# A decoder step on one core: the sample's attention in even steps, with four 32-column tiles in place of two of 64

## The chip, the cores and the metric

The kernel runs on one core of a Trainium2 chip. The metric is the device time of one execution in microseconds (us), lower is better; the time of a kernel is the median of its runs. The engines of the core that appear below are TensorE (PE; its weight loads are listed apart as PEld), VectorE (DVE), ScalarE (ACT), GpSimd (POOL) and SyncE (SP, which here issues every DMA).

## The reference

One layer of a decoder for a prompt of 512 tokens and for a sample group of 8 sequences with 8 new tokens each, after 2048 past tokens. Both share the weights. All is float32.

```python
z = rms(x) @ w_in                               # 9776 columns: q, k/v, gates, RNN inputs
# A) sparse attention, 16 heads of 64, 4 key/value heads
k_c, v_c = compress(past, 32 -> 1)              # 64 compressed blocks of the past
o_cmp, imp = softmax(q @ k_c) @ v_c             # imp: which blocks matter
idx = top_k(imp, 15)                            # of 32 blocks of 64 keys
o_sel = softmax(q @ [k[idx], k_new]) @ [v[idx], v_new]
o_win = softmax(q @ [last 512 keys, k_new]) @ ...
o_att = g0 * o_cmp + g1 * o_sel + g2 * o_win    # gates per head
# B) RG-LRU recurrence; then both are projected, gated, merged, projected again
y = x + (sig(gm_att) * ((o_att * silu(g_att)) @ w_att_out) + sig(gm_rnn) * u_rnn) @ w_out
```

For the sample group, per sequence ("batch" below): 16 heads x 8 tokens = 128 query rows; 2048 past keys in pages of 128, of which the selected blocks count, 512 window keys and 8 new ones.

## The kernel before

**The main stream.** TensorE works through the weights in column tiles of 128. A slot is half the rows of such a tile for half of the 576 tokens: 8 steps of three matmuls, 24 in all (L1609 to L1611: each weight and each input is split into two parts, high and low, of the faster float32r type). ACT makes the high part of a weight (L225, `whi`), DVE the low one (L231, `wlo`), and SP loads the weight after the next (L218, `raw`) as soon as the low part is done. The remaining work of the kernel is inserted between slots, and, for the sample's attention, also in the middle of a slot.

**The order.** The program sets the order itself (`manual_schedule`): on each engine instructions stand as the code states them. The sample's attention is a list of events with a time each (`sample_events`, by the numbers of `SCH`); `sample_steps` executes those of one time and tells by a cost estimate how far it has come. `sample_work` calls it until that share catches up with the share of the slots that lie between the end of the prompt's attention and the RNN. It is called at the beginning and in the middle of each slot.

**One batch.** All 128 query rows share the partitions. Keys lie as [64 dims of two key heads, keys], so that a pair `c` of key heads is one matmul: its weights are 64 query columns (2 heads x 32 rows, zero where the head does not match), its moving side 256 keys (`s_scores`, L904). The pair c=0 writes partitions 0 to 63, c=1 64 to 127; these are the 64-column tiles. The operands are true float32, and such a matmul shows in the trace as two instructions, two passes.

- `c_square` to `x_select`: norm of the compressed keys, their scores (`m<-skvx,qb`), softmax, sum over heads (L930), choice of blocks as a bias per block.
- `k_load`, `v_load`: keys and values by pages, on SP's queue, in pieces of 256 keys.
- `k_scores`, `k_max`: scores of 512 keys (a "part", n2 = 0 to 3 past, 4 window) into a bank `s`; DVE adds the bias, copies to SBUF and takes the maximum.
- `s_softmax`, `s_exp`, `s_scale`, `p_scale`: when all five parts have their maxima, one maximum for each of the two softmaxes; ACT exponentiates; sums, reciprocal and gate make one factor per row, with which POOL scales the probabilities.
- `s_turn`, `s_turned`: four 128 x 128 transposes on TensorE (`t`, L1023), copied out by ACT (`spt`).
- `s_out`: probabilities (64 columns of a pair) times values (128 columns: both heads of the pair, of which each row needs one), L1052, all added up in one bank `o`, the new and compressed keys' first (`vx`).
- `s_sum`, `s_fin`, `s_put`: copy, transpose, and the wanted halves into `osm`.

A batch's scores begin 38 event times after its own beginning, its values 66, and batches follow every 22, so that values of one batch and scores of a later one alternate.

Of the kernel before, what the change touches and what calls it, by code (L numbers as in the profile page):

```python
# [10 lines left out]
F = mybir.dt.float32  # L11
# [5 lines left out]
VLAG = 2  # L17
KEPT = 3
NORM = 15
BASE = 2.0  # L20
# [5 lines left out]
CF, PG = 18, 25  # L26
YSTD = 4
SCH = 22, 38, 66, 5
# [13 lines left out]
TINY = 1e-30  # L42
# [5 lines left out]
def _constants():  # L48
# [26 lines left out]
    add("zero", np.zeros((128, 1)))  # L75
    return np.concatenate(cols, 1)
# [37 lines left out]
def nsa_rglru_step(ctx, tc, a, o):  # L114
# [714 lines left out]
    def q_batch(x):  # L829

        x.q = pp["s"].tile([128, 2, 64], F, tag="qb", name="qb", bufs=2)
        G.memset(x.q, 0.0)
        for c in range(2):
            for gl in range(2):
                me = slice(gl * 64, gl * 64 + 64)
                V.tensor_copy(x.q[me, c, gl * 32:gl * 32 + 32].rearrange("p (r t) -> p r t", t=8), zs[me, c, :, x.b:64:8])
# [29 lines left out]
    def c_reduce(x, n):  # L866
        if n == 0:
            x.kvx = pp["a"].tile([128, 4, 80], F, tag="skvx", name="skvx", bufs=3)
# [5 lines left out]
    def c_fetch(x):  # L874
        if x.b >= KEPT:
            x.kvx = pp["a"].tile([128, 4, 80], F, tag="skvx", name="skvx", bufs=3)
            S.dma_start(x.kvx[:, :, 8:72], kc_d[x.b])
# [23 lines left out]
    def s_scores(dst, x, k):  # L901

        for c in range(2):
            T.matmul(dst[c * 64:c * 64 + 64], x.q[:, c], k(c), start=True, stop=True)  # L904

    def x_scores(x):

        m = bank("m")
        s_scores(m[:, :80], x, lambda c: x.kvx[:, c, :])
        x.m = m  # L910

    def x_exp(x):
        m = held_bank("m", x.m)
        x.e = pp["s"].tile([128, 80], F, tag="se", name="se", bufs=3)
        x.sm = pp["s"].tile([128, 24], F, tag="ssm", name="ssm", bufs=3)
        sm = x.sm
        V.tensor_add(x.e[:, 0:8], m[:, 0:8], C("snew"))
        V.tensor_add(x.e[:, 72:80], m[:, 72:80], C("snew"))
        V.tensor_reduce(sm[:, 0:1], m[:, 8:72], axis=AX.X, op=OP.max, negate=True)
        A.activation(x.e[:, 8:72], m[:, 8:72], AF.Exp, bias=sm[:, 0:1], accum_out=sm[:, 1:2])  # L920

    def x_prob(x):
        sm = x.sm
        V.tensor_scalar_max(sm[:, 1:2], sm[:, 1:2], TINY)
        V.reciprocal(sm[:, 1:2], sm[:, 1:2])
        V.tensor_scalar_mul(x.e[:, 8:72], x.e[:, 8:72], sm[:, 1:2])

    def x_sum(x):
        m = bank("m")
        T.matmul(m[:, :64], C("rsum"), x.e[:, 8:72], start=True, stop=True)  # L930
        x.m = m

    def x_select(x):
# [12 lines left out]
        V.tensor_scalar_mul(x.e[:, 8:72], x.e[:, 8:72], gR[:, 0, x.b:x.b + 1])  # L946

    kraw, vraw = {}, {}

    def k_load(x, n):  # L950
        t = pp["s"].tile([128, 2, 256], F, tag="kr", name="kr", bufs=6)
        if n < 8:
            for k in range(2):
                S.dma_start(t[:, :, k * 128:k * 128 + 128],
                            a["selk"][ds(page(x.b, 2 * n + k, "k"), 1)].rearrange("o p c f -> p (o c) f"))
        else:
            S.dma_start(t, a["wink"][x.b, :, :, (n - 8) * 256:(n - 8) * 256 + 256])
        kraw[x.b, n] = t

    def v_load(x, n):  # L960
        t = ap.tile([128, 2, 256], F, tag="q", name="vr", bufs=8)
        if n < 8:
            for k in range(2):
                S.dma_start(t[:, k], a["selv"][ds(page(x.b, 2 * n + k, "v"), 1)].rearrange("o p f -> p (o f)"))
        else:
            S.dma_start(t, a["winv"][x.b, :, (n - 8) * 2:(n - 8) * 2 + 2])
        vraw[x.b, n] = t

    def k_scores(x, n2):

        x.s = bank("s")
        for n in (2 * n2, 2 * n2 + 1):
            t = kraw.pop((x.b, n))
            s_scores(x.s[:, n % 2 * 256:n % 2 * 256 + 256], x, lambda c: t[:, c])

    def k_max(x, n2):
        s, sm = held_bank("s", x.s), x.sm
        p = pp["s"].tile([128, 512], F, tag="p2", name="sp", bufs=2) if (x.b * 5 + n2) % 8 > 5 else \
            pp["a"].tile([128, 512], F, tag="p", name="sp", bufs=6)
        x.P[n2] = p  # L980
        if n2 < 4:
            V.tensor_tensor_reduce(p.rearrange("p (n k) -> p n k", k=64), s.rearrange("p (n k) -> p n k", k=64),
                                   x.bias[:, n2 * 8:n2 * 8 + 8, None].to_broadcast([128, 8, 64]), 1.0, -3.0e38,
                                   OP.add, OP.max, sm[:, 4 + n2:5 + n2])
        else:
            V.tensor_tensor_reduce(p[:, :8], s[:, :8], C("wm"), 1.0, -3.0e38, OP.add, OP.max, sm[:, 9:10])
            V.tensor_tensor_reduce(p[:, 8:], s[:, 8:], C("zero").to_broadcast([128, 504]), 1.0, -3.0e38, OP.add, OP.max, sm[:, 11:12])

    def s_softmax(x):

        sm, e = x.sm, x.e
        V.tensor_reduce(sm[:, 8:9], e[:, 0:8], axis=AX.X, op=OP.max)
        V.tensor_reduce(sm[:, 10:11], e[:, 72:80], axis=AX.X, op=OP.max)
        V.tensor_reduce(sm[:, 2:3], sm[:, 4:9], axis=AX.X, op=OP.max, negate=True)
        V.tensor_reduce(sm[:, 3:4], sm[:, 9:12], axis=AX.X, op=OP.max, negate=True)

    def s_exp(x, n2):
        sm, e = x.sm, x.e
        if n2 < 5:
            p = x.P[n2]  # L1000
            A.activation(p, p, AF.Exp, bias=sm[:, 3:4] if n2 == 4 else sm[:, 2:3],
                         accum_out=sm[:, 12 + n2:13 + n2] if n2 < 4 else sm[:, 17:18])
        else:
# [708 lines left out]
```

## Time and profile before

| | |
|---|---|
| median of 3 runs | 1703.17 us (1701.27 to 1703.93) |
| profiled execution | 1700.71 us, span 1698.9 us |
| TensorE busy | 1673.2 us (98%), 12645 matmuls |
| DVE / ACT / POOL busy | 1027.0 / 747.8 / 348.6 us |
| TensorE clock granted | 0.997 of full |
| HBM | 155 GB/s over the span |

The span is the time from the first to the last instruction; the execution's own time is 1.8 us more. Busy time counts instructions that overlap only once. A matmul's recorded duration includes its way through the array, so matmuls that start every 0.13 us each last about 0.3; how fast they follow each other is read from their starts. In a row of the timeline come start, duration, engine, line, operation, output and inputs, shapes, and how many equal instructions were put together. "Idle before" and "<-" name what an engine waited for. The sample's attention runs from about 723 to 1056 us of the span.

### The profile page before, as it was taken

What the parts mean: (1) busy time and instruction counts of PE and PEld (TensorE: products, weight loads), DVE (VectorE), ACT (ScalarE), POOL (GpSimd) and SP (SyncE); (2) the same over time, 40 slices, a digit from 0 to 9 for tenths busy, and PEclk for the clock granted to TensorE, in tenths of its full rate; (3) what the DMA queues carried; (4) which work ended last, traced back from release to release, by engine and by line L of the source; (5) the groups of instructions that cost most, each with busy time, mean ns of one, the idle gap of its engine ahead of it and who ended that gap; (6) DMA issues with size and microseconds to landing.
All of it is one profiled execution on the core that took longest, in us unless ns stands there. A gap on an engine that the chain in (4) does not pass through costs nothing.

```text
span 1698.9 us, 32907 instructions
## 1 busy us (share of the span) xinstructions
PE 1673.2 (98%) x12645; PEld 1599.3 (94%) x12645; DVE 1027.0 (60%) x2117; ACT 747.8 (44%) x1361; POOL 348.6 (21%) x423
## 2 busy tenths in 40 slices
PE   9989999999999999999999999999999999999999
PEld 8989999998998999988888889999999999999999
DVE  6767768778776876443333422656655334448785
ACT  6354553554455454343444432566664122233332
POOL 0014443533543444310011020000003011110000
PEclk9999999999999999999999999999999999999999
DMA  6247534533543444366676654322227444556442
GB/s 223 76 169 243 182 112 134 164 103 116 165 135 104 149 149 136 120 191 212 209 216 196 206 177 133 100 79 83 79 89 242 138 153 142 166 183 227 154 136 81
DMA packets 147455, 257.93 MB, mean 152 GB/s; under 512 B 19937, under 2 KB 80482, under 8 KB 147042
## 3 DMA queue, kind: packets, MB, share of 16 engines
q1 hardware_dynamic: 147298, 255.82, 46.6%
q8 instruction: 100, 1.64, 0.4%
q14 instruction: 57, 0.47, 0.1%
HBM read 228.08 MB, written 36.07 MB: 155 GB/s over the span
## 4 chain that ended last, share of the span: by engine, by line
PE 81%; DVE 10%; ACT 6%; issue 2%; DMA 1%; SPq 0%; POOL 0%; ACTq 0%; POOLq 0%; DVEq 0%
PE g L1609 21%; PE g L1610 20%; PE g L1611 20%; PE o L1052 3%; PE s L904 2%; DVE wlo L231 2%; PE g L1386 1%; PE g L1384 1%; PE g L1385 1%; PE t L737 1%; DVE pt L741 1%; DVE p L718 1%; ACT p L722 1%; ACT whi L225 1%; PE t L1023 1%
## 5 line engine op out<-in xcount | busy, mean ns | idle before, releaser
L1609 PE MATMUL g<-xh,whi 128*128 128x288 f32 x2368 | 716.5, 303 | 0.1
L1611 PE MATMUL g<-xh,wlo 128*128 128x288 f32 x2368 | 698.9, 295 | 1.1 <-DVE wlo L231 1.1
L1610 PE MATMUL g<-xl,whi 128*128 128x288 f32 x2368 | 699.1, 295 | 0.0
L1609 PEld LDWEIGHTS g<-xh,whi 128*128 128x128 f32 x2368 | 446.1, 188 | 22.2 <-issue 19.6
L1610 PEld LDWEIGHTS g<-xl,whi 128*128 128x128 f32 x2368 | 446.1, 188 | 1.3
L1611 PEld LDWEIGHTS g<-xh,wlo 128*128 128x128 f32 x2368 | 445.7, 188 | 1.3 <-DVE wlo L231 1.3
L231 DVE TENSOR_TENSOR wlo<-raw,whi 128x1024 fp32r<-128x1024 f32 x192 | 257.2, 1340 | 98.6 <-ACT whi L225 98.1
L225 ACT ACTIVATE whi<-raw 128x1024 fp32r<-128x1024 f32 x192 | 202.2, 1053 | 116.8 <-PE g L1610 111.9
L864 POOL TENSOR_TENSOR cr<-cr,wcs 128x512 f32<-128x512 f32 x128 | 182.8, 1433 | 158.4 <-DMA cr<-in_cmp 133.2
L722 ACT ACTIVATE p<-p,sm,rq 128x128 f32<-128x128 f32 (+3 forms) x128 | 82.8, 648 | 150.2 <-DVE sm L719 150.0
L730 POOL TENSOR_SCALAR p<-p,sm 128x128 f32<-128x128 f32 (+3 forms) x128 | 68.7, 549 | 211.9 <-DVE sm L727 94.7
L741 DVE TENSOR_TENSOR pt<-t,pt 128x512 fp32r<-128x512 f32 x96 | 66.1, 689 | 65.0 <-ACT pt L740 63.7
L870 DVE TENSOR_REDUCE skvx<-cr 128x16 f32<-128x512 f32 x128 | 86.7, 677 | 0.4
L1017 POOL TENSOR_SCALAR sp<-sp,ssm 128x512 f32<-128x512 f32 x40 | 30.9, 789 | 262.0 <-DVE ssm L1012 224.0
L740 ACT ACTIVATE pt<-t 128x512 fp32r<-128x512 f32 x96 | 56.5, 592 | 57.4 <-PE t L737 56.6
L571 ACT ACTIVATE mh<-ur 128x288 fp32r<-128x288 f32 x32 | 14.2, 445 | 145.0 <-POOL ur L565 145.0
L1611 PE MATMUL g<-oah,wlo 128*128 128x288 f32 x256 | 75.5, 295 | 0.0
L1611 PE MATMUL g<-hrh,wlo 128*128 128x288 f32 x256 | 75.5, 295 | 0.0
L1610 PE MATMUL g<-oal,whi 128*128 128x288 f32 x256 | 75.4, 295 | 0.0
L1609 PE MATMUL g<-oah,whi 128*128 128x288 f32 x256 | 75.4, 294 | 0.0
L1610 PE MATMUL g<-hrl,whi 128*128 128x288 f32 x256 | 75.3, 294 | 0.0
L1609 PE MATMUL g<-hrh,whi 128*128 128x288 f32 x256 | 75.3, 294 | 0.0
(377 smaller groups left out, 2967.5 us busy)
## 6 DMA issues: line engine op xcount, KB each, us to landing
raw<-in_w_in SPq DMA_DIRECT2D x152, 512.0 KB, 3.4
cr<-in_cmp SPq DMA_DIRECT2D x128, 256.0 KB, 3.4
kr<-in_selk SPq DMA_DIRECT2D x128, 128.0 KB, 3.1
vr<-in_selv SPq DMA_DIRECT2D x128, 128.0 KB, 3.4
tg<-gm SPq DMA_DIRECT2D x32, 288.0 KB, 4.4
tgi<-tg SPq DMA_DIRECT2D x32, 288.0 KB, 4.2
yr<-in_w_out SPq DMA_DIRECT2D x18, 512.0 KB, 4.7
raw<-in_w_rnn SPq DMA_DIRECT2D x16, 512.0 KB, 4.2
```

The source lines that it names most:

```text
L225: A.activation(hi, raw[k], AF.Copy)
L231: V.tensor_sub(lo, raw.pop(k), hi.bitcast(F))
L722: A.activation(p[:, :n], p[:, :n], AF.Exp, bias=sm[:, 1, r - r0:r - r0 + 1], scale=rq[:, i, r:r + 1], accum_out=sm[:, 2, r - r0:r - r0 + 1])
L730: G.tensor_scalar(p[:, :n], p[:, :n], sm[:, 3, r - r0:r - r0 + 1], 1.0, op0=OP.mult, op1=OP.mult)
L740: A.activation(hi, t, AF.Copy)
L741: V.tensor_sub(lo, t, hi.bitcast(F))
L864: G.tensor_tensor(v, v, wcs[:, :, None, :].to_broadcast([128, 4, 4, 32]), op=OP.mult)
L870: V.tensor_reduce(x.kvx[:, :, 8 + n * 4:12 + n * 4], v, axis=AX.X, op=OP.add)
L1052: T.matmul(ob[c * 64:c * 64 + 64, :128], pt[rows, k, c], v[rows, u, c * 128:c * 128 + 128], start=n < 0, stop=n == 9 and u == 1, skip_grou ...
L1609: T.matmul(gb[:, :HF], wh[:, k, :], r_h[:, hs], start=kk == 0, stop=False)
L1610: T.matmul(gb[:, :HF], wh[:, k, :], r_l[:, hs], start=False, stop=False)
L1611: T.matmul(gb[:, :HF], wl[:, k, :], r_h[:, hs], start=False, stop=last and k == 7)
```

## The change

Four things change together.

1. **Tiles.** The query weights become [128, 4, 32]: one key head each, with 32 query columns. `s_scores` issues four matmuls of 512 keys, whose results lie on partitions 0, 32, 64 and 96. `s_out` issues, for 128 keys, four matmuls of 32 columns with only the 64 value columns of that head. The result of a part is [128, 64].
2. **Softmax by parts.** Each part of 512 keys takes its own maximum (the negative, as a minimum) and is exponentiated at once, without waiting for the others. The values of each part go into their own 64 columns of bank `o`, eight in all: four past parts, new keys, window, window's new keys, compressed keys. At the end factors exp(max of part - max of all), times the gate and over the sum, weigh the eight (`s_factors`, `s_total`, `s_sum`). The scaling of probabilities on POOL is gone. The new and compressed keys' probabilities are turned in one go and masked into three copies (`x_turned`, constant `xm`), with three times four matmuls (`x_out`).
3. **Order.** `sample_steps` states 52 even steps: batch b starts at step 6 + 5b; part n2 is loaded three steps ahead (values: at the step itself), scored at t, turned at t + 2, and used at t + 3. Within a step the transposes come first, then the values, then the scores. `sample_work` is called once a slot, and a step is never split.
4. **Memory.** Keys come in tiles of 512 (4 buffers); the pool of the prompt's attention is closed before the sample's opens.

```diff
@@ q_batch
-        x.q = pp["s"].tile([128, 2, 64], F, tag="qb", name="qb", bufs=2)
+        x.q = pp["s"].tile([128, 4, 32], F, tag="qb", name="qb", bufs=3)
...
@@ s_scores
-        for c in range(2):
-            T.matmul(dst[c * 64:c * 64 + 64], x.q[:, c], k(c), start=True, stop=True)
+        for h in range(4):
+            T.matmul(dst[h * 32:h * 32 + 32], x.q[:, h], k(h // 2), start=True, stop=True)
...
+    def x_out(x):
+        ob = held_bank("o", x.o)
+        for n, part in enumerate((4, 6, 7)):
+            for h in range(4):
+                T.matmul(ob[h * 32:h * 32 + 32, part * 64:part * 64 + 64], x.pt[:80, n * 128 + h * 32:n * 128 + h * 32 + 32],
+                         x.pt[:80, 384 + h * 64:448 + h * 64], start=True, stop=True)
...
@@ k_load
-        t = pp["s"].tile([128, 2, 256], F, tag="kr", name="kr", bufs=6)
+        t = x.K[n2] = pp["s"].tile([128, 2, 512], F, tag="kr", name="kr", bufs=4)
...
@@ s_exp
-            A.activation(p, p, AF.Exp, bias=sm[:, 3:4] if n2 == 4 else sm[:, 2:3],
-                         accum_out=sm[:, 12 + n2:13 + n2] if n2 < 4 else sm[:, 17:18])
+        p, n = x.P[n2], n2 + n2 // 4
+        A.activation(p, p, AF.Exp, bias=x.sm[:, NM + n:NM + n + 1], scale=-1.0, accum_out=x.sm[:, SUM + n:SUM + n + 1])
...
-    def p_scale(x, n2):
-        G.tensor_scalar(x.P[n2], x.P[n2], x.sm[:, 23:24] if n2 == 4 else x.sm[:, 22:23], 1.0, op0=OP.mult, op1=OP.mult)
...
@@ s_out
-            for c in range(2):
-                T.matmul(ob[c * 64:c * 64 + 64, :128], pt[rows, k, c], v[rows, u, c * 128:c * 128 + 128],
-                         start=n < 0, stop=n == 9 and u == 1, skip_group_check=True)
+        for k in range(4):
+            for h in range(4):
+                T.matmul(ob[h * 32:h * 32 + 32, at_:at_ + 64], pt[:, k, h * 32:h * 32 + 32], v[k // 2][:, k % 2, h * 64:h * 64 + 64],
+                         start=k == 0, stop=k == 3)
...
@@ s_sum
-        x.t2 = etile("t2")[:, :128]
-        A.activation(x.t2, held_bank("o", x.o)[:, :128], AF.Copy)
+        V.tensor_mul(t, ob, x.sm[:, FAC:FAC + 8, None].to_broadcast([128, 8, 64]))
+        V.tensor_reduce(x.t2, t.rearrange("p n d -> p d n"), axis=AX.X, op=OP.add)
...
@@ sample_steps
+            s = 6 + 5 * x.b
...
+            for n2 in range(5):
+                t = s + n2
+                put(t - 3, 0, k_load, x, n2)
+                put(t, 0, v_load, x, n2)
+                put(t, 4, k_scores, x, n2)
+                put(t, 8, k_max, x, n2)
+                put(t, 9, s_exp, x, n2)
+                put(t + 2, 1, s_turn, x, n2)
+                put(t + 2, 6, s_turned, x, n2)
+                put(t + 3, 2, s_out, x, n2)
+            put(s + 3, 3, x_out, x)
...
@@ main loop
-                sample_work(s + 0.5)
+                sample_work(s + 1)
...
-            if step == 4 and ssteps is not None and s < slot_of[first_r]:
-                sample_work(s + 1)
```

How this moves instructions on TensorE, in the middle of the sample's attention. Before, values of one batch and scores of a later one; the rows left out are 12 projection matmuls each time:

```order
L1052 MATMUL o<-vr,spt 64x128 x4
L1023 MATMUL t<-cst,sp 128x128 x4
...
L1052 MATMUL o<-vr,spt 64x128 x4
L904 MATMUL s<-kr,qb 64x256 x4
L904 MATMUL m<-skvx,qb 64x80 x2
```

Now, about the same place; the rows left out are 24 projection matmuls:

```order
L1021 MATMUL t<-cst,sp 128x128 x4
L957 MATMUL t<-cst,se 80x128
L959 MATMUL t<-cst,skvx 80x128 x2
L1035 MATMUL o<-vr,spt 32x64 x16
L902 MATMUL s<-kr,qb 32x512 x4
...
L1021 MATMUL t<-cst,sp 128x128 x4
L887 MATMUL m<-ssq,cst 128x128
L1035 MATMUL o<-vr,spt 32x64 x16
L902 MATMUL s<-kr,qb 32x512 x4
```

Full-width transposes come first, and then all tiled matmuls of the step in one run, a whole slot apart from the next. (`order` names are those of the profile: `o`, `s`, `t`, `m` are banks, `vr` and `kr` values and keys, `spt` turned probabilities, `qb` queries.)

The second place is SP's queue, where the keys and values of a step are issued. Before (a row without tile names is a register instruction):

```order
L964 DMA vr<-in_selv 128x256
L954 ISA
L954 DMA kr<-in_selk 128x2x128
L954 ISA
L954 DMA kr<-in_selk 128x2x128
L218 DMA raw<-in_w_in 128x1024
L964 ISA
L964 DMA vr<-in_selv 128x256
```

Now:

```order
L991 ISA
L991 DMA vr<-in_selv 128x256
L981 ISA
L981 DMA kr<-in_selk 128x2x128
L981 ISA
L981 DMA kr<-in_selk 128x2x128
L981 ISA
L981 DMA kr<-in_selk 128x2x128
L981 ISA
L981 DMA kr<-in_selk 128x2x128
L216 DMA raw<-in_w_in 128x1024
```

Four value loads and four key loads of a step follow each other; a weight load, which waits for DVE's `wlo`, stands behind them and ahead of the next step's loads.

More of the change, by code (lines that the diff above doesn't have):

```diff
@@ L75, in _constants @@
     add("zero", np.zeros((128, 1)))
+    add("xm", np.stack([p < 8, (p >= 72) & (p < 80), (p >= 8) & (p < 72)], 1))
     return np.concatenate(cols, 1)
@@ L867, in c_reduce @@
         if n == 0:
-            x.kvx = pp["a"].tile([128, 4, 80], F, tag="skvx", name="skvx", bufs=3)
+            x.kvx = pp["x"].tile([128, 4, 80], F, tag="skvx", name="skvx", bufs=3)
         v = x.cr.pop(n).rearrange("p c (n j) -> p c n j", j=32)
@@ L875, in c_fetch @@
         if x.b >= KEPT:
-            x.kvx = pp["a"].tile([128, 4, 80], F, tag="skvx", name="skvx", bufs=3)
+            x.kvx = pp["x"].tile([128, 4, 80], F, tag="skvx", name="skvx", bufs=3)
             S.dma_start(x.kvx[:, :, 8:72], kc_d[x.b])
@@ new lines, in x_turn_, with x_turned @@
+    def x_turn_(x):
+        t = x.tx = bank("t")
+        T.transpose(t[:80, 0:128], x.e, ident)
+        for c in range(2):
+            T.transpose(t[:80, 128 + c * 128:256 + c * 128], x.kvx[:, 2 + c, :], ident)
+    def x_turned(x):
+        t = held_bank("t", x.tx)
+        x.pt = pp["s"].tile([128, 640], F, tag="vx", name="vx", bufs=2)
+        for n in range(3):
+            A.activation(x.pt[:80, n * 128:n * 128 + 128], t[:80, :128], AF.Copy, scale=C("xm")[:80, n:n + 1])
+        A.activation(x.pt[:80, 384:], t[:80, 128:384], AF.Copy)
@@ L954, in k_load @@
                 S.dma_start(t[:, :, k * 128:k * 128 + 128],
-                            a["selk"][ds(page(x.b, 2 * n + k, "k"), 1)].rearrange("o p c f -> p (o c) f"))
+                            a["selk"][ds(page(x.b, 4 * n2 + k, "k"), 1)].rearrange("o p c f -> p (o c) f"))
         else:
[L957 to L967, printed above, removed]
+            S.dma_start(t, a["wink"][x.b])
@@ L969, in k_scores, with v_load @@
+    def v_load(x, n2):
+        t = x.V[n2] = [ap.tile([128, 2, 256], F, tag="q", name="vr", bufs=8) for _ in range(2)]
+        for k in range(2):
+            if n2 < 4:
+                for i in range(2):
+                    S.dma_start(t[k][:, i], a["selv"][ds(page(x.b, 4 * n2 + 2 * k + i, "v"), 1)].rearrange("o p f -> p (o f)"))
+            else:
+                S.dma_start(t[k], a["winv"][x.b, :, 2 * k:2 * k + 2])
     def k_scores(x, n2):
         x.s = bank("s")
-        for n in (2 * n2, 2 * n2 + 1):
-            t = kraw.pop((x.b, n))
-            s_scores(x.s[:, n % 2 * 256:n % 2 * 256 + 256], x, lambda c: t[:, c])
+        t = x.K.pop(n2)
+        s_scores(x.s, x, lambda c: t[:, c])
@@ L1126, in sample_steps @@
-    def sample_steps():
-        ev = sample_events()
-        steps = {t: [] for t in range(ev[0][0], ev[-1][0] + 1)}
-        for t, _, _, f, args in ev:
-            steps[t].append((f, args))
-        heavy = (k_max, s_turned)
-        cost = [BASE + sum(0.6 if f in heavy else 0.1 for f, _ in fs) for fs in steps.values()]
-        done = 0.0
-        for c, fs in zip(cost, steps.values()):
-            for f, args in fs:
+            s = 6 + 5 * x.b
+            put(s - 6, 0, c_fetch, x)
+            put(s - 4, 9, q_batch, x)
@@ L1136, in sample_steps @@
+            put(s + 3, 3, x_out, x)
+            put(s + 5, 9, s_factors, x)
+            put(s + 6, 7, s_total, x)
+            put(s + 7, 7, s_sum, x)
+            put(s + 10, 1, s_fin, x)
+            put(s + 10, 7, s_put, x)
+        for t in range(max(steps) + 1):
+            for _, _, f, args in sorted(steps.get(t, []), key=lambda e: e[:2]):
                 f(*args)
-            done += c
-            yield done / sum(cost)
+            yield (t + 1) / (max(steps) + 1)
     rp_ = {}
```

196 lines of the change are left out of this document (78 added, 118 removed).

## The prediction

> **What bounds the kernel now.** I read the page's shares and chain of waits first, to learn which engine sets the end.
>
> ```profile
> PE 1673.2 (98%) x12645; PEld 1599.3 (94%) x12645; DVE 1027.0 (60%) x2117; ACT 747.8 (44%) x1361; POOL 348.6 (21%) x423
> ...
> PE 81%; DVE 10%; ACT 6%; issue 2%; DMA 1%; SPq 0%; POOL 0%; ACTq 0%; POOLq 0%; DVEq 0%
> ```
>
> TensorE is busy for 98% of the span, and the chain that ends last is 81% TensorE. What counts is therefore how long TensorE needs for the sample's attention. Next come the stretch in which that attention runs and a piece behind it with projections alone (busy time by window: PE, PEld, DVE, ACT, POOL, clock, DMA share, GB/s), and TensorE's groups of instructions in the stretch.
>
> ```profile
> 723.00:1056.00 333.00, 331.84 (x2753) 282.83 (x2752) 119.95 (x427) 130.45 (x276) 36.18 (x71) 1.00 0.63 194
> 1060.00:1080.00 20.00, 20.00 (x153) 20.00 (x152) 10.99 (x30) 6.38 (x12) 0.24 (x1) 1.00 0.33 106
> ```
>
> ```profile
> L1609 PE MATMUL g<-xh,whi 128*128 128x288 f32 x502 | 158.7, 316 | 0.0
> L1610 PE MATMUL g<-xl,whi 128*128 128x288 f32 x503 | 148.1, 294 | 0.0
> L1611 PE MATMUL g<-xh,wlo 128*128 128x288 f32 x502 | 147.7, 294 | 0.0
> ...
> L904 PE MATMUL s<-kr,qb 128*64 128x256 f32 x320 | 42.4, 385 | 1.2 <-DMA kr<-in_selk 1.2
> ```
>
> In 333.0 us TensorE waits 1.2 us; its clock is full (1.00). The 502 + 503 + 502 = 1507 projection matmuls stay. Their durations (294 to 316 ns) overlap, so a cost has to be read from the distance between starts: in the second window 153 ran in 20 us, two or three of them begun before it, so one starts every 0.133 us. That is what the timeline of TensorE shows around single "excursions", as I call an insertion of attention work between two projection matmuls. One with values alone:
>
> ```profile
> 870.02 0.29 PE L1611 MATMUL g<-xh,wlo 128*128 128x288 f32 x1
> 870.25 0.66 PE L1052 MATMUL o<-vr,spt 128*64 128x128 f32 x8
> 870.84 0.40 PE L1609 MATMUL g<-xh,whi 128*128 128x288 f32 x1
> 871.07 0.29 PE L1610 MATMUL g<-xl,whi 128*128 128x288 f32 x1
> ```
>
> From 870.02 to the second one after the excursion, 871.07, are 1.05 us; two projections' distances (0.27) are in it, so eight value instructions cost 0.78 us. The same for values, scores and the compressed keys' scores (m) together:
>
> ```profile
> 852.77 0.29 PE L1611 MATMUL g<-xh,wlo 128*128 128x288 f32 x1
> 853.00 0.66 PE L1052 MATMUL o<-vr,spt 128*64 128x128 f32 x8
> 853.48 1.03 PE L904 MATMUL s<-kr,qb 128*64 128x256 f32 x8
> 854.35 0.31 PE L904 MATMUL m<-skvx,qb 128*64 128x80 f32 x4
> 854.59 0.40 PE L1609 MATMUL g<-xh,whi 128*128 128x288 f32 x1
> 854.83 0.30 PE L1610 MATMUL g<-xl,whi 128*128 128x288 f32 x1
> ```
>
> For scores alone:
>
> ```profile
> 737.76 0.29 PE L1611 MATMUL g<-xh,wlo 128*128 128x288 f32 x1
> 737.98 1.08 PE L904 MATMUL s<-kr,qb 128*64 128x256 f32 x8
> 738.99 0.40 PE L1609 MATMUL g<-xh,whi 128*128 128x288 f32 x1
> 739.23 0.29 PE L1610 MATMUL g<-xl,whi 128*128 128x288 f32 x1
> ```
>
> And for transposes alone:
>
> ```profile
> 864.78 0.29 PE L1611 MATMUL g<-xh,wlo 128*128 128x288 f32 x1
> 864.91 0.60 PE L1023 MATMUL t<-cst,sp 128*128 128x128 f32 x4
> 865.27 0.38 PE L1609 MATMUL g<-xh,whi 128*128 128x288 f32 x1
> 865.49 0.29 PE L1610 MATMUL g<-xl,whi 128*128 128x288 f32 x1
> ```
>
> Same arithmetic. All three together: 2.06 - 0.27 = 1.79. Scores alone: 1.47 - 0.27 = 1.20. Transposes: 0.71 - 0.27 = 0.44. Values plus scores plus m, less values, leave 1.01 for scores and m; the starts divide it (853.48 to 854.35): 0.87 for scores, 0.14 for m. Scores alone cost 1.20, so about **0.34 us of each excursion is no work at all**. It goes with 64-column tiles: transposes, full width like the projections, have none of it (four at 0.11). Without it eight value instructions take 0.44: four pairs, 0.11 each, the two tiles side by side. The waits of the weight loads show it too:
>
> ```profile
> PEld g L1609 <- issue: 19.6, 76, 0.4
> ...
> PEld o L1052 <- issue: 11.6, 69, 0.2
> ```
>
> Each time the shape switches, in or out, the weight load waits for nothing that is recorded.
>
> **The change part by part.** The built order counts, before: 108 excursions, 101 with 64-column tiles; 40 runs of scores (two key tiles each), 80 of values. After: 47, of which 44 have 32-column tiles. One excursion holds four transposes, the values of a whole 512-key part, then its scores.
>
> Before, from unit prices: scores 40 x 0.865 = 34.6; values 80 x 0.44 = 35.2; the new keys' values, 16 pairs x 0.11 = 1.8; 192 transposes x 0.11 = 21.1; the two small sums, 32 x 0.11 = 3.5; m 16 pairs x 0.07 = 1.1; switching 101 x 0.345 = 34.8. Sum 132.1. Check: 333.0 - 1507 x 0.133 = 132.6, the 1.2 of waiting included. The prices hold.
>
> After:
> - *Switching* goes from 101 to 44: 15.2, **saved 19.6**. No row has a switch to 32 columns. Bounds: the 0 that transposes show (saving 15 more) and double (15 lost). I take the 0.345 of the nearest row.
> - *Scores*: four tiles of 512 keys in two passes, where two tiles of 256 keys took four. If four tiles run side by side as two do, 34.6 again: 0.
> - *Values*: a head's weights now meet only its own 64 columns, not 128. Per part 8 groups of four instructions instead of 8 pairs, at half the length: 0.055 instead of 0.11, so 40 x 0.44 = 17.6: **saved 17.6**. Bounds: 0.055 and the old 0.11 (0 saved). Nearest is m's pair of 80 columns at 0.07 with new weights each time, so short streams do scale: I take 0.055.
> - *New keys' values*, now three masked copies: 8 x 6 x 0.055 = 2.6 for 1.8: 0.8 lost.
> - Transposes, small sums, m: the same counts, 0.
> - *Feeding of instructions.* A part's values and scores are 40 loads and 40 matmuls within about 1.3 us. How fast the sequencer hands over is seen where its queue was empty: the first two loads of a scores run, usual and after a DMA wait:
>
> ```profile
> 730.61 0.14 PEld L904 LDWEIGHTS s<-kr,qb 128*64 128x64 f32 x2 [0.16 <-issue]
> ...
> 732.39 0.17 PEld L904 LDWEIGHTS s<-kr,qb 128*64 128x64 f32 x2 [1.58 <-DMA kr<-in_selk]
> ```
>
> Usually the second load begins 0.01 us after the first, here 0.035: one matmul of the program (two passes) per 0.035 us. A part's 16 value matmuls then need 16 x 0.035 = 0.56 against 0.44 of work, and some stand queued behind the transposes. Scores wait for up to four DMAs, so the last tile may start late. Between 0 and 0.14 per part, 0 to 5.6 in all; I take 1.5.
>
> *What is moved off TensorE.* The five scalings on POOL go; a product and a sum over parts (s_sum) and small factors come to DVE, a few exponentials to ACT. In the window row DVE is busy 120.0 and ACT 130.5 of 333.0: cover enough at 298. The tightest new distance is from the compressed scores to their sum (x_sum), one slot of 24 projections later, 3.2 us:
>
> ```profile
> 854.56 0.69 DVE L982 CUSTOM_DVE_ANT_1 sp<-s,sbias 128x512 f32<-128x512 f32 x1 [4.47 <-PE s L904]
> ...
> 856.49 0.26 DVE L926 TENSOR_SCALAR se<-se,ssm 128x64 f32<-128x64 f32 x1
> ```
>
> From the end of the scores to the last operation's end are 2.2 us: hidden. If that cover went, 8 waits of about 1 us. The key loads, queued on SP, now all stand within steps 3 to 45 of 52, and behind them, on the same queue, the weights' loads, which wait for DVE. The issue of four key loads, and the largest of SP's waits in the stretch:
>
> ```profile
> 862.16 2.83 SPq L954 DMA_DIRECT2D kr<-in_selk  x4
> ...
> SPq L218 <- DVE wlo L231: 60.9, 20, 9.1
> ```
>
> All its waits there add to 89.3, so it issues for 333 - 89 = 244 us. Eight of the 16 loads of window keys are merged away (8 x 0.7, about -6). The new stretch is 200.4 + 98 = 298 us, and 43/52 of it, 246, must hold some 238. It fits, barely, with loads three steps (17 us) ahead: I take 0.
>
> Sum after: 15.2 + 34.6 + 17.6 + 2.6 + 21.1 + 3.5 + 1.1 + 1.5 = 97.2, and 0.5 for waits: 97.7. Saved 132.6 - 97.7 = **34.9 us**. The profiled execution took 1700.71 us (span 1698.9 plus 1.8), 2.5 under the median of 1703.17. It should become 1666, the median **1668**.
>
> **Rivals.**
> *SP becomes the bound.* A key load's issue (2.83 / 4 = 0.71 us) may stretch once the same bytes move in less time (194 GB/s would be 217). With 6% more, SP needs 252 for the 246, and with the weights' loads waiting in line another 4 (an estimate: one slot of 24 projections and little more): about 10 us late, **1678**. For: 97% occupancy. Against: the waits of 89 us show slack that moves along.
>
> *Values do not shrink.* If a group costs 0.11 whatever its length: 17.6 + 2.6 lost, **1688**. For: pairs of 128 columns and one load of 128 (the transposes) both take 0.11, so a load may be the floor. Against: m's 0.07. The Trainium skill (TensorEngine Tiling (Array Packing), Instruction Overhead) warns not to tile a dimension that is already small, since a matmul of one column takes as long as one of about 60. By that rule 64 columns lie just above the floor, and the sum stays 1668.
>
> *Slower: instructions are fed one pass per 0.035 us.* Place: each part's 32 value passes. Price: 32 x 0.035 = 1.12 for 0.44, 0.68 x 40 = 27; the new keys' values 0.5 x 8 = 4; the last score tile 0.2 x 40 = 8: 39 in all, **1707**. It decides above 0.031 per pass, where 35 us are used up. For: the row at 732.39. Against: there two tiles, thus two program matmuls, lie 0.035 apart. The Trainium skill (TensorE: Matmul & The Clock Gate, "Wait — 56ns, not 53.3ns?") gives a floor of about 25 ns between starts; by it, an estimate, 1685; the loads 0.01 apart above say otherwise for different tiles.
>
> *Slower: the four tiles run two by two.* Scores double (+34.6), values keep 0.11 (+17.6), new keys' and m +3.7: 56, **1724**. It decides where four streams are stretched by over 35/56, 63%. For: no row with four. Against: two tiles cost each other nothing.
>
> **How the numbers follow.** Forecast 1668, own range 1660 to 1675: 0.60. SP 0.14; values not shorter 0.10; feeding 0.07, half of it at a milder price near 1690; two by two 0.09. The range is 1658 to 1690: the first three cases, less their tails, about 0.8. About 0.2% (3.4 us) is what a measurement of this kernel can tell from no change. Faster: 0.60 + 0.14 + 0.10 + 0.03 = 0.87; within 0.2%: 0.03; slower 0.10.
>
> **What would show it.** In the profile after: an excursion of transposes, values and scores costs 0.44 + 0.44 + 0.87 + 0.34 = 2.1 us by the same arithmetic; groups of four value instructions 0.055 apart; scores' second pass 0.43 after the first; PEld's "issue" waits halved; SP's waits on DVE down from 61. Wrong if TensorE waits for kr or vr by more than a few us, if a values run lasts over 0.6, or if four starts are not within 0.03 us.

## The result and the profile after

The changed kernel takes 1664.57 us (median of 4 runs, 1663.31 to 1666.82), the kernel before 1702.81 beside it: the ratio is 0.9777, with a 95% interval of 0.9761 to 0.9794. The forecast was 1668 us. 38.2 us are saved where 34.9 were forecast. The profiled execution took 1663.31 us, with a span of 1661.4 (1700.71 and 1698.9 before).

The page of the changed kernel, busy time by engine and the chain that ended last:

```profile
PE 1635.9 (98%) x13477; PEld 1571.3 (95%) x13477; DVE 1035.4 (62%) x2125; ACT 754.7 (45%) x1393; POOL 315.7 (19%) x383
...
PE 82%; DVE 9%; ACT 6%; issue 2%; DMA 1%; POOL 0%; SPq 0%; ACTq 0%; DVEq 0%; POOLq 0%
```

TensorE runs 832 matmuls more and is busy 37.3 us less: 1635.9 for 1673.2. It is still the chain. POOL lost the scalings (348.6 to 315.7), DVE and ACT gained 8 and 7 us, behind TensorE. Next the stretch with the sample's attention in two views, busy time by window and TensorE's groups by shape:

```profile
723.00:1020.00 297.00, 296.67 (x3602) 256.99 (x3602) 131.02 (x448) 140.48 (x312) 4.16 (x26) 1.00 0.71 217
```

```profile
L1599 PE MATMUL g<-xh,whi 128*128 128x288 f32 x508 | 154.5, 304 | 0.0
L1601 PE MATMUL g<-xh,wlo 128*128 128x288 f32 x507 | 149.3, 294 | 0.0
L1600 PE MATMUL g<-xl,whi 128*128 128x288 f32 x507 | 149.3, 294 | 0.0
L902 PE MATMUL s<-kr,qb 128*32 128x512 f32 x320 | 41.9, 595 | 0.0
L1035 PE MATMUL o<-vr,spt 128*32 128x64 f32 x1280 | 26.2, 222 | 0.0
...
L902 PE MATMUL m<-skvx,qb 128*32 128x80 f32 x64 | 2.7, 234 | 0.3 <-DVE skvx L897 0.3
```

By the forecast's arithmetic: 297.0 less 1522 projections at 0.133 is 94.6 us of attention (forecast 97.7, before 132.6). TensorE waits 0.3 us in the whole stretch, and not for keys (kr) or values (vr). One excursion in TensorE's timeline:

```profile
849.08 0.29 PE L1601 MATMUL g<-xh,wlo 128*128 128x288 f32 x1
849.21 0.60 PE L1021 MATMUL t<-cst,sp 128*128 128x128 f32 x4
849.74 0.65 PE L1035 MATMUL o<-vr,spt 128*32 128x64 f32 x32
850.21 0.52 PE L973 MATMUL o<-vx 80*32 80x64 f32 x24
850.54 1.05 PE L902 MATMUL s<-kr,qb 128*32 128x512 f32 x8
851.41 0.33 PE L902 MATMUL m<-skvx,qb 128*32 128x80 f32 x8
851.67 0.40 PE L1599 MATMUL g<-xh,whi 128*128 128x288 f32 x1
851.91 0.30 PE L1600 MATMUL g<-xl,whi 128*128 128x288 f32 x1
```

From 849.08 to 851.91, less two distances of 0.133, are 2.56 us for transposes, values of 512 keys, the new keys' values, scores of 512 keys and m. The values take 0.47 (849.74 to 850.21) before the next begins, the scores 0.87 (850.54 to 851.41). Before, 108 excursions held the work of 40 parts, 2.7 for each; now 47 do.

### The profile page after: what moved, and what is told of

Read it like the earlier page. It is cut to its first block, busy times and chain, and to the rows that moved or that the text cites. A ratio compares the mean times of both kernels' runs of the same rounds, so it can differ in the third digit from the quotient of the medians.

```text
span 1661.4 us, 34484 instructions
## 1 busy us (share of the span) xinstructions
PE 1635.9 (98%) x13477; PEld 1571.3 (95%) x13477; DVE 1035.4 (62%) x2125; ACT 754.7 (45%) x1393; POOL 315.7 (19%) x383
## 4 chain that ended last, share of the span: by engine, by line
PE 82%; DVE 9%; ACT 6%; issue 2%; DMA 1%; POOL 0%; SPq 0%; ACTq 0%; DVEq 0%; POOLq 0%
PE g L1599 21%; PE g L1601 20%; PE g L1600 20%; PE s L902 2%; PE t L735 2%; DVE wlo L229 2%; PE g L1375 2%; PE g L1377 2%; PE g L1376 2%; PE o L1035 1%; ACT whi L223 1%; DVE p L716 1%; DVE pt L739 1%; ACT p L720 1%; PE t L1021 1%
## 5 line engine op out<-in xcount | busy, mean ns | idle before, releaser
L1005 DVE CUSTOM_DVE_ANT_1 sp<-s,sbias 128x512 f32<-128x512 f32 x32 | 22.1, 689 | 60.1 <-PE s L902 60.1
```

## Experiments

Each time stands against the changed kernel's 1664.57 us or the 1701.7 to 1702.8 of the kernel before, which ran beside every one. The intervals reach 2 to 3 us to either side, so a difference of 1 or 2 us between two rows shows nothing. "A run" is an unbroken row of column-tile matmuls on TensorE, between two instructions of full width; the built order counts 106 runs in the kernel before, 44 in the changed one. An "excursion" is a trip out of the projections, as in the prediction; one may hold several runs.

| kernel | median us | ratio to before, 95% | change |
|---|---|---|---|
| each step split in two | 1678.67 | 0.9865 (0.9848 to 0.9881) | +14.1 on changed |
| values twice | 1681.21 | 0.9877 (0.9861 to 0.9894) | +16.6 on changed |
| scores in 64 columns | 1669.35 | 0.9805 (0.9789 to 0.9822) | +4.8 on changed |
| all in 64 columns | 1687.01 | 0.9911 (0.9894 to 0.9929) | +22.4 on changed |
| values head by head | 1693.16 | 0.9945 (0.9927 to 0.9963) | +28.6 on changed |
| key loads halved | 1695.90 | 0.9972 (0.9955 to 0.9989) | +31.3 on changed |
| before, one call a slot | 1696.40 | 0.9969 (0.9956 to 0.9981) | -6.1 on before |
| before, transposes first | 1690.84 | 0.9940 (0.9922 to 0.9958) | -12.0 on before |
| two parts in a run | 1684.75 | 0.9904 (0.9886 to 0.9922) | +20.2 on changed |
| changed, keys fetched late | 1689.28 | 0.9927 (0.9912 to 0.9943) | +24.7 on changed |
| two parts, fetch early | 1662.99 | 0.9769 (0.9755 to 0.9783) | -1.6 on changed |
| the same, two slots later | 1656.85 | 0.9737 (0.9724 to 0.9750) | -7.7 on changed |

The theory: the time is TensorE's, and the gain has two parts, fewer switches in and out of column tiles and value matmuls of half the length. The rivals of the first four runs: the switches are hidden, or the instructions are fed too slowly.

### Each step split in two

```diff
-            for _, _, f, args in sorted(steps.get(t, []), key=lambda e: e[:2]):
-                f(*args)
-            yield (t + 1) / (max(steps) + 1)
+            evs_ = sorted(steps.get(t, []), key=lambda e: e[:2])
+            for half in (0, 1):
+                for order, _, f, args in evs_:
+                    if (order >= 4) == half:
+                        f(*args)
+                yield (t + 1) / (max(steps) + 1)
```

> The changed kernel with each step of the sample cut in two: the new-key work, the transposes and the values at the slot's start, the scores in the middle of the slot. The same instructions, but 81 trips into column tiles instead of 44. Theory (a trip costs 0.34 us on TensorE, whatever it holds): 37 x 0.34 = 12.6 us more than the changed kernel's 1664.6, so 1677 us, 0.985 of the kernel before. Rival (a trip is hidden and the gain came from the shorter value matmuls and elsewhere): 1664 to 1666 us.

1678.67 us: 14.1 us for 37 runs more, 0.38 each. 1.4 of it is a single wait that the changed kernel does not have (TensorE's sum over heads, for DVE, at 735.4 us); without it 12.7 remain, 0.34 each. A switch is paid, at 32 columns as at 64.

### Values twice

```diff
-        for k in range(4):
+        for k in (0, 1, 2, 3, 0, 1, 2, 3):
             for h in range(4):
```

> The changed kernel with the value matmuls of each 512-key part issued twice into the same place, the second time starting the sum anew, so the result is unchanged: 64 instead of 32 matmul instructions in a run. Theory (four tiles side by side, a group of four each 0.055 us): 8 groups x 0.055 = 0.44 us in each of 40 runs, 17.6 us more, 1682 us. Rival (the run of 32 was short only because its instructions lay ready; the supply gives one in 0.035 us): up to 32 x 0.035 = 1.12 us in each run, 45 us more, 1709 us. Between the two, the excess over 17.6 us is the price of feeding.

1681.21 us: 16.6 us for 40 times 8 groups more, 0.052 us a group. In its timeline the 64 value instructions of a run take 0.92 us to the next start (842.74 to 843.65), 0.45 more than 32 of them: 0.056 a group. A second half of 32 instructions right behind the first thus costs 0.45 where 0.44 was expected. Nothing that can be told from zero is left for feeding; the rival's 45 us are out.

### Scores in 64 columns

```diff
-        for h in range(4):
-            T.matmul(dst[h * 32:h * 32 + 32], x.q[:, h], k(h // 2), start=True, stop=True)
+        for c in range(2):
+            T.matmul(dst[c * 64:c * 64 + 64], x.q[:, c * 2:c * 2 + 2].rearrange("p h n -> p (h n)"), k(c), start=True, stop=True)
```

> The changed kernel with the scores in two 64-column tiles, as in the kernel before, the values still in four 32-column tiles. Theory (8 score instructions take 0.87 us in either shape, since as many columns stream through; only entering and leaving column tiles costs, not a change of their width): 1664.6 us within 2 us. Rival (each change of tile width drains as a trip's edge does, half of 0.34 us): one change more in each of 40 trips, 7 us more, 1671.5 us; if it costs as much as a whole trip, 14 us more, 1678 us.

1669.35 us, 4.8 more: neither the theory's 0 nor the rival's 7. The timelines of TensorE show where, first the changed kernel, then this one:

```profile
841.25 0.65 PE L1035 MATMUL o<-vr,spt 128*32 128x64 f32 x32
841.72 1.04 PE L902 MATMUL s<-kr,qb 128*32 128x512 f32 x8
```

```profile
845.09 0.65 PE L1035 MATMUL o<-vr,spt 128*32 128x64 f32 x32
845.67 1.08 PE L902 MATMUL s<-kr,qb 128*64 128x512 f32 x4
```

The same values; the scores start 0.58 us after them instead of 0.47. So a change of tile width inside a run does cost 0.11 us, about a third of a switch to full width, and the scores end 0.04 later. The theory was wrong there. The change had not run into this price, since all its column tiles have one width.

### All in 64 columns

```diff
-            for h in range(4):
-                T.matmul(ob[h * 32:h * 32 + 32, at_:at_ + 64], pt[:, k, h * 32:h * 32 + 32], v[k // 2][:, k % 2, h * 64:h * 64 + 64],
-                         start=k == 0, stop=k == 3)
+            for r in range(2):
+                for c in range(2):
+                    T.matmul(ob[c * 64:c * 64 + 64, at_:at_ + 64], pt[:, k, c * 64:c * 64 + 64],
+                             v[k // 2][:, k % 2, (2 * c + r) * 64:(2 * c + r) * 64 + 64],
+                             start=k == 0 and r == 0, stop=k == 3 and r == 1)
```

The scores change as above, the new keys' values in the same way.

> The changed kernel's order with the tile shape of the kernel before: scores, values and the new keys' values all in two 64-column tiles, 44 runs of column-tile work as in the changed kernel. (Left out: the values of two heads are summed in one place of 64 columns, so the output is not the reference's; the number of matmul instructions and of streamed columns in them is that of 64-column tiles.) Theory (pairs instead of fours side by side, 0.055 us each): 8 groups x 0.055 = 0.44 us in 40 runs, 17.6 us, and 0.33 us in 8 runs of new keys' values, 2.6 us: 20.2 us more than the changed kernel, 1685 us, which leaves 106 - 44 = 62 runs x 0.345 = 21 us as the gain of the order alone. Rival (the width of the tiles is worth nothing, the whole gain is the order): 1665 us.

1687.01 us. TensorE's timeline:

```profile
844.73 1.15 PE L1037 MATMUL o<-vr,spt 128*64 128x64 f32 x32
845.71 1.03 PE L902 MATMUL s<-kr,qb 128*64 128x512 f32 x4
```

A part's values last 0.98 us to the next start, not 0.47. 40 x 0.51 = 20.4, and 2.6 for the new keys' values, are 23.0; measured 22.4. (In the kernel before, a pair of value instructions streams 128 columns, here twice as many pairs stream 64 each. A part takes about the same: two runs of 0.48 there, 853.00 to 853.48 above.) This divides the gain of 38.2 us: 15.6 remain with the new order in the old tiles, and in these 15.6 the new keys' values run in pairs, by the expected price 2.6 dearer than in the changed kernel. **The order is worth 18.2 us, the tiles of 32 columns for the past keys' values 19.8**, each to within the 3 us of the intervals. For the order 21 were expected.

### The kernel before with one call a slot, and with its transposes first

The first calls `sample_work` once in a slot:

```diff
-                sample_work(s + 0.5)
+                sample_work(s + 1)
...
-            if step == 4 and ssteps is not None and s < slot_of[first_r]:
-                sample_work(s + 1)
```

> The kernel before with its sample called once in a slot instead of twice, and nothing else: 64-column tiles, parts of 256 keys, and 59 trips into column tiles instead of 101. Theory: 42 x 0.345 = 14.5 us less than the kernel before, 1688 us, 0.9915. Rival 1 (the trips' price is not the cause; the gain needs the 32-column values): 1703 us. Rival 2 (work put closer together waits for its own banks and transposed copies, which takes the gain back): 1700 us or more, with TensorE waits on the o and t banks in the trace.

1696.40 us, 6.1 less and not 14.5, and TensorE waits only 0.2 us in the stretch: neither theory nor a rival. The timeline of TensorE shows what the count of excursions had missed:

```profile
810.32 0.66 PE L1052 MATMUL o<-vr,spt 128*64 128x128 f32 x8
810.90 0.66 PE L1023 MATMUL t<-cst,sp 128*128 128x128 f32 x4
811.49 0.66 PE L1052 MATMUL o<-vr,spt 128*64 128x128 f32 x8
811.98 1.03 PE L904 MATMUL s<-kr,qb 128*64 128x256 f32 x8
```

One excursion, but full-width transposes stand between two runs, and there is a toll around them too: transposes begin 0.58 us after the values (0.49 where scores follow), the next values 0.59 after the transposes (0.44 for four of them), 0.09 + 0.15 = 0.24 in all. Counted by runs there are 88, 18 fewer than the 106 of the kernel before: 18 x 0.345 = 6.2, measured 6.1. The next kernel tests that count. It adds, in each call, the transposes ahead of the rest:

```diff
+        for first in (True, False):
+            for f, args in due:
+                if (f.__name__ == "s_turn") == first:
+                    f(*args)
```

(Some transposes then read probabilities before they are final, so one output is not the reference's; the instructions and their sizes are the same.)

> The kernel before with its sample called once in a slot, and in each call the transposes of the probabilities ahead of everything else: 59 trips out of the projections as in the kernel that is only called once, but 69 runs of column-tile work instead of its 88 and the 106 of the kernel before, since no transpose stands between two of them. Theory (the unit of the price is the run of column-tile instructions, entered from any full-width one, not the trip out of the projections): 37 x 0.345 = 12.8 us less than the kernel before, 1689.8 us, and 6.6 us less than the kernel called once. Rival (the trip is the unit, and the kernel called once lost 8 us elsewhere): no gain over that kernel, 1696 us.

1690.84 us, 12.0 less than the kernel before: 37 runs fewer, 0.32 each. The excursions with column tiles are 59 in both kernels, and still 5.6 us lie between them for 19 runs, 0.29 each (4.9 us by the ratios to the kernel before). The excursion is not the unit; the run is. That a run between transposes costs less than one between projections, 0.24 and about 0.34, is read from the timelines; the times are not fine enough to tell it.

### Values head by head

```diff
-        for k in range(4):
-            for h in range(4):
+        for h in range(4):
+            for k in range(4):
```

> The changed kernel with the loops of the value matmuls exchanged: four key blocks of one head after each other, then the next head, so that eight neighbouring instructions go to the same 32-column tile. Same instructions, same result. Theory A (side by side needs instructions for different tiles within the few that wait at TensorE; the run of one tile, 8 x 0.055, must end first, partly overlapped by the next head's): between 0.5 and 1.3 us more in each of 40 runs, 20 to 52 us, 1685 to 1717 us. Theory B (TensorE takes them out of order as tiles come free): 0, 1665 us.

1693.16 us: 0.72 us more for each part, with the same instructions. In its timeline:

```profile
848.80 1.23 PE L1035 MATMUL o<-vr,spt 128*32 128x64 f32 x29
849.82 0.63 PE L902 MATMUL s<-kr,qb 128*32 128x512 f32 x3
849.87 0.33 PE L1035 MATMUL o<-vr,spt 128*32 128x64 f32 x3
850.03 1.02 PE L902 MATMUL s<-kr,qb 128*32 128x512 f32 x5
```

Two things are seen. The last values start 1.07 us after the first, where in the changed kernel the whole run took 0.47. And three scores, which the program has behind all values, start before the last three values: matmuls of free tiles pass those that wait for theirs, but evidently not from far behind, or the order of the loops would cost nothing. Four tiles side by side come from neighbouring instructions for different tiles. That the loop over heads is the inner one is thus worth 28.6 us.

### Key loads halved

```diff
-                S.dma_start(t[:, :, k * 128:k * 128 + 128],
-                            a["selk"][ds(page(x.b, 4 * n2 + k, "k"), 1)].rearrange("o p c f -> p (o c) f"))
+                pg = page(x.b, 4 * n2 + k, "k")
+                for c in range(2):
+                    S.dma_start(t[:, c, k * 128:k * 128 + 128],
+                                a["selk"][ds(pg, 1)].rearrange("o p c f -> p (o c) f")[:, c])
```

> The changed kernel with each page of keys fetched by two transfers instead of one, the same bytes: 128 issues more on SyncE. The forecast took SyncE's 238 us of issuing in the sample's stretch at no cost; its waits there are 63 us of 297. Theory (TensorE does not wait for it): 128 x 0.5 = 64 us more issuing just fills the waits, 0 to 10 us more, at most 1675 us. Rival (SyncE was already the bound, every issue is paid): 64 to 96 us more, 1729 us or above.

1695.90 us, 31.3 more, between the two. SP's waits for DVE (total, times, longest), first of the changed kernel in the whole stretch, 723 to 1020 us, and in its part up to the last load of a page of keys, 723 to 961 us; then of this kernel up to its last such load, 723 to 1002 us:

```profile
SPq L216 <- DVE wlo L229: 41.2, 15, 9.8
```

```profile
SPq L216 <- DVE wlo L229: 11.0, 10, 1.9
```

```profile
SPq L216 <- DVE wlo L229: 3.4, 2, 3.2
```

And this kernel's waits of TensorE in 723 to 1020 us:

```profile
PE m L887 <- ACT ssq L879: 9.1, 4, 3.0
PE s L902 <- DMA kr<-in_selk: 6.6, 4, 3.3
PE s L902 <- DMA kr<-in_wink: 0.9, 1, 0.9
```

All of SP's waits in the changed kernel's stretch sum to 62.9 us, but 45 of these lie behind the last page of keys. Up to it SP waits 17.8 of 238 us and is at work for 220; here it waits 17.4 of 279 us and is at work for 262. The halved loads thus gave SP some 41 us more to do, not the estimated 64, and none of it came out of SP's waits; three quarters of it came out as time. The theory, that the issues fill the waits, was wrong. SP did not hold TensorE up in the changed kernel (0.3 us of waits there), but while keys are loaded it has next to no room, which makes the rival right in kind and too high in price.

Here TensorE waits 16.6 us by the rows, for keys and for squares (ACT waits 14.9 us for the fetch of what it squares). Some 3 us go to a lower granted clock: 0.96 in 800 to 840 and in 960 to 1000 us, where the changed kernel has 1.00. The other 11 were not taken apart.

### Two parts in a run

If a run is the unit, 23 of them should beat 44. The order of the changed kernel's `put` lines, with the column-tile work of two parts at even slots and the transposes and sums at odd ones:

```diff
+        def when(j):
+            return 6 + j // 2 * 2
...
-            s = 6 + 5 * x.b
+            odd = x.b % 2
+            s, last = when(5 * x.b), when(5 * x.b + 4)
             put(s - 6, 0, c_fetch, x)
...
-            put(s - 4, 9, c_square, x)
-            put(s - 3, 1, c_norm, x)
...
+            put(s - 6, 9, c_square, x)
+            put(s - 5, 1.5, c_norm, x)
...
-                t = s + n2
...
+                j = 5 * x.b + n2
+                t = when(j)
...
                 put(t, 4, k_scores, x, n2)
...
-                put(t + 2, 1, s_turn, x, n2)
...
-                put(t + 3, 2, s_out, x, n2)
...
+                put(t + 3, 1 + j % 2 * 0.1, s_turn, x, n2)
...
+                put(t + 4, 5.5 if odd and n2 == 0 else 2, s_out, x, n2)
```

Here j is a part's number, `5 * x.b + n2`; scores stay at t.

> The changed kernel with the column-tile work of two 512-key parts put into one run every second slot, and the transposes and small sums into the slots between: 23 runs instead of 44, the same instructions. Theory (a run costs 0.345 us, whatever it holds): 21 x 0.345 = 7.2 us less than the changed kernel, 1657.4 us. Rival 1 (two parts at once make the scores wait for banks or for keys, or the softmax of two parts late): 1664 us or more, with TensorE waits in the trace. Rival 2 (a longer run of small instructions outruns their supply, so each costs more): the gain halves, 1661 us.

1684.75 us, 20.2 more. The waits of TensorE and of ACT in 723 to 1020 us, and one window (the granted clock stands third from the end), in this kernel and in the changed one:

```profile
PE m L887 <- ACT ssq L879: 16.4, 6, 4.6
```

```profile
ACT ssq L879 <- DMA skvx<-kc: 28.7, 5, 7.7
```

```profile
920.00:960.00 40.00, 35.37 (x407) 32.04 (x400) 19.11 (x81) 19.12 (x48) 0.00 (x0) 0.91 0.72 217
```

```profile
920.00:960.00 40.00, 40.00 (x504) 34.19 (x503) 19.21 (x67) 20.62 (x50) 0.00 (x0) 1.00 0.78 236
```

The fault was a detail of the new order, not the runs: the squares (`c_square`) had come into the slot in which their keys are fetched (`c_fetch`), so ACT waited 28.7 us for five loads and TensorE 16.4 us for ACT, with a lower clock around it. Two kernels separate this. The first moves only that fetch in the changed kernel:

```diff
-            put(s - 6, 0, c_fetch, x)
+            put(s - 4, 0, c_fetch, x)
```

> The changed kernel with one line changed: the compressed keys are fetched two slots later, in the slot of their squares, as in the order with two parts. 44 runs as in the changed kernel. Theory (the late fetch alone costs what that order lost): 5 loads with some 3 us of waiting each and the clock lost around them, 15 to 27 us more than the changed kernel, 1680 to 1692 us. Rival (the fetch lands in time, the crowding was the cause): 1665 us.

1689.28 us: the late fetch alone costs 24.7 us, with more scatter than elsewhere (1682.14 to 1691.11). The profiled execution is the fastest of these, 18.8 us above the changed kernel's, and TensorE waits 14.7 us for the squares in it. The second moves the fetch of the order with two parts forward:

```diff
-            put(s - 6, 0, c_fetch, x)
+            put(max(0, s - 9), 0, c_fetch, x)
```

> The kernel with two parts in one run every second slot, with one line changed: a sample's compressed keys are fetched three slots earlier (the fetch had stood in the same slot as the squares that ScalarE makes of it; in the changed kernel two slots lie between). Theory (that order's loss of 20 us was the fetch: TensorE's 16.4 us of waiting for the squares, and the lower granted clock around each wait): the waits go, 23 runs instead of 44 remain, 21 x 0.345 = 7.2 us less than the changed kernel, 1657.4 us. Rival (two parts at once crowd ScalarE and VectorE, whatever the fetch): 1670 us or more.

1662.99 us: 21.8 gained back, but 5.6 of the 7.2 us are still missing. One wait is left, at the first batch, in its timeline:

```profile
722.16 0.49 PE L887 MATMUL m<-ssq,cst 128*128 128x128 f32 x2 [2.48 <-ACT ssq L879]
...
723.15 0.44 PE L1605 MATMUL g<-xl,whi 128*128 128x288 f32 x1
723.39 0.44 PE L1606 MATMUL g<-xh,wlo 128*128 128x288 f32 x1
...
726.03 0.41 PE L1605 MATMUL g<-xl,whi 128*128 128x288 f32 x1
726.27 0.30 PE L1606 MATMUL g<-xh,wlo 128*128 128x288 f32 x1
726.41 0.30 PE L1604 MATMUL g<-xh,whi 128*128 128x288 f32 x1
```

After the wait the projections start 0.24 us apart, until 726.27, and then 0.14 and less. The granted clock (third from the end) was 0.50 in this time:

```profile
722.90:726.30 3.40, 3.40 (x17) 3.40 (x16) 2.61 (x4) 2.10 (x3) 1.14 (x8) 0.50 0.02 5
```

The last kernel puts all of the sample but the fetches two slots later (`8 + j // 2 * 2`).

> The kernel with two parts in one run and the early fetch, with everything of the sample but the fetches two slots later, so that the first batch's squares, which wait for the attention's last transfer, are not needed by TensorE at once. In the kernel without this shift TensorE waited 2.48 us for them at 719.7 us, and the projections behind that wait came 0.24 instead of 0.133 us apart for 3.6 us, 1.6 us more. Theory (only that wait stands between that kernel and its 23 runs): 4.1 us less than its 1663.0 us, 1659 us, 0.9743 of the kernel before, about 5.5 us below the changed kernel. Rival (the sample then ends later, or the time comes back elsewhere): 1663 us.

1656.85 us, **7.7 us less than the changed kernel**, 45 less than the kernel before, and 6.1 less than without the shift: the wait's 4.1, and 2 more. 1.1 of these 2 lie between the medians of the kernel before that ran beside the two (1702.80 and 1701.68). The profiled executions also differ by something that the shift does not touch: in the one without it the granted clock was 0.50 in 269 to 272 us, long before the sample, and 1.00 in the last kernel's. By the ratios to the kernel before, the gain over the changed kernel is 6.8 us and not 7.7. The last kernel's window, and one of its excursions with two parts:

```profile
723.00:1020.00 297.00, 296.67 (x3653) 265.10 (x3652) 135.04 (x469) 139.08 (x313) 4.34 (x27) 1.00 0.71 219
```

```profile
840.09 1.10 PE L1035 MATMUL o<-vr,spt 128*32 128x64 f32 x64
841.00 1.91 PE L902 MATMUL s<-kr,qb 128*32 128x512 f32 x16
842.72 0.34 PE L902 MATMUL m<-skvx,qb 128*32 128x80 f32 x8
...
846.29 1.03 PE L1021 MATMUL t<-cst,sp 128*128 128x128 f32 x8
```

64 values in 0.91 us, 16 scores in 1.72: twice one part's, at half as many switches. 21 runs fewer, 0.37 each (0.32 by the ratios).

## Why the prediction was right, step by step

**TensorE alone sets the time.** Right. The stretch shrank by the sum of its excursions, and the engines that took work on did not show up in TensorE's waits.

**Switching, 0.345 us each, 101 to 44, 19.6 us saved.** The mechanism and the price hold: 0.34, 0.32 and 0.37 us a run where 37, 37 and 21 were added or taken away, and the 32-column tiles pay it like those of 64. The unit was named wrongly: the prediction counted excursions with column tiles, where runs have to be counted; the kernel with one call a slot came out 8 us off for that reason. In the change itself it hardly mattered (106 to 44 for 101 to 44), since 5 excursions of the kernel before held a second run. The order alone was worth 18.2 us, near the forecast's 19.6 - 0.8 (the new keys' values). In part that is luck: the forecast counted too few (57 for 62), and the 18.2 + 0.8 are 0.31 a run where it took 0.345.

**Scores, 0 saved.** Right: 0.87 us for 512 keys in either shape, second passes 0.43 behind the first. The rival with four tiles two by two (1724) is out.

**Values, 17.6 saved.** Right in kind, 2.2 short: 19.8, by the kernel with all tiles at 64 columns. A part takes 0.47 in the changed kernel, 2 x 0.48 in the kernel before and 0.98 in that with all tiles at 64, a saving of about 0.5 and not 0.44. The prediction had taken the pair's 0.11 and its half. A run takes a little more than its groups (0.48 for 4 x 0.11, 0.47 for 8 x 0.055), and the kernel before had two runs for each part. The rival that values do not shrink (1688) is out.

**Feeding, 1.5 us and up to 5.6 within the sum, 39 in the rival.** Mis-sized: doubled runs of values cost 0.052 us a group by the times and 0.056 by the timeline, against the 0.055 of the columns, so the row that it was read from, a second load 0.035 us behind the first after a wait, told nothing about a running stream. The term should have been 0.

**SP, 0.** Right: TensorE waits for no keys or values, and the rival (1678) is out. SP is at work for 297 - 63 = 234 us in the stretch, forecast 238. It was as near as it was called: up to the last page of keys SP is at work for 220 of 238 us, and with halved loads 41 us more of work there cost 31.3.

**The sum.** 34.9 forecast (19.6 + 17.6 - 0.8 - 1.5), 38.2 measured. One kernel divides this gain into 18.2 and 19.8, so that these two add up to it (38.0) is no second proof. The values' 2.2 and the feeding's 1.5, less 0.6 of the order, are the difference.

**The signs named ahead.** An excursion of transposes, values and scores costs 2.07 us (2.1 named, at 767.96 us); the groups (0.056 apart), the passes (0.43), the short values run (0.47 to the next start; the row's 0.65 includes the last matmul's own 0.22) and SP's largest wait (41.2, from 60.9) came as named. One sign failed: PEld's "issue" waits were to be halved. They are fewer, but longer:

```profile
PEld g L1599 <- issue: 26.0, 31, 0.8
PEld o L1035 <- issue: 4.2, 24, 0.2
```

30.2 us in 55 waits, for 31.2 in 145 before by the two rows of the prediction; with the smaller rows of this kind it is 35.0 in 71 for 37.8 in 184. The first row's mean rose from 0.26 to 0.84 us. What ends such a wait is not recorded; that it now holds the long last pass of the scores, whose four loads are done at its start, is only argued. These rows locate switches, but are not their price.

## What to carry to other kernels

Count the unbroken runs of column-tile matmuls in the built order, not the trips: each cost 0.3 to 0.4 us here whatever it held, so full-width instructions belong beside a run and never inside it, and longer runs of one tile width are the next gain. Inside a run put instructions for different tiles next to each other. When such an order is rewritten, look at what each moved step waits for: one fetch two slots too late cost 24.7 us, three times what longer runs gained.

## What the runs showed of the hardware that was not expected

**A change of tile width** inside a run cost 0.11 us, a third of a switch to full width. The Trainium skill (TensorEngine Tiling (Array Packing), Key Properties) says that changing the tiling mode drains TensorE. The runs agree in so far as each change costs time, 0.11 us for 32 to 64 columns and about 0.34 us for a whole run's way in and out of full width; no row shows the drain itself.

**A short wait can cost more than itself.** After 2.48 us without matmuls the granted clock was 0.50, and the projections came 0.24 us apart from 722.91 to 726.27, 14 times 0.107 us lost, 1.5 us. The length of the wait does not decide it. After a longer one, in the changed kernel with the late fetch, the granted clock was 1.00:

```profile
814.44 0.49 PE L887 MATMUL m<-ssq,cst 128*128 128x128 f32 x2 [3.28 <-ACT ssq L879]
```

```profile
814.40:818.00 3.60, 3.56 (x55) 2.61 (x56) 2.39 (x4) 2.12 (x4) 0.00 (x0) 1.00 0.86 278
```

And in the kernel with two parts in a run and the fetch not yet moved, two waits for the same squares, of 2.54 us until 804.51 and of 2.49 us until 873.83, were followed by clocks of 0.53 and 1.00:

```profile
804.50:808.00 3.50, 3.49 (x15) 3.49 (x16) 0.51 (x3) 3.48 (x7) 0.00 (x0) 0.53 0.64 184
873.80:877.00 3.20, 3.17 (x24) 3.17 (x25) 0.51 (x3) 3.18 (x7) 0.00 (x0) 1.00 0.64 194
```

The Trainium skill (TensorE: Matmul & The Clock Gate, What's actually happening) has the clock halved after an idle window of some 3.4 us that runs freely. Half speed agrees with the trace, and so does a part of chance; but 2.48 us is less than that window, and 3.28 did not bring it on.

**Matmuls start out of the program's order.** With values head by head, three scores started at 849.82 us, before the last three values, at 849.87.
